# A two-layer hybrid block taken by halves of the tokens, with its norms by Newton's steps and its silu by tanh

## The chip, the core and the metric

The kernel runs on one core of a Trainium2 chip. The metric is the device time of one execution in microseconds. The core has five engines with queues of their own: TensorE (PE, with its weight loads shown apart as PEld), VectorE (DVE), ScalarE (ACT), GpSimd (POOL) and SyncE (SP), which issues most of the loads. An engine takes its instructions in order and waits at semaphores for the others.

## What is computed

A first block (attention beside a state-space layer, then a feed-forward of retrieved experts) takes 512 tokens of width 1024. Nothing of it is changed. Its output goes through the second block, two layers of this:

```python
def hybrid_layer(x, ...):
    x = x + 0.5 * swiglu(rmsnorm(x, ffn1_norm), ffn1_gate, ffn1_up, ffn1_down)
    z = rmsnorm(x, mix_norm) @ w_in
    (aq, ak, av, iq, ik, iw, bq, bk, bv, bg, br, cu, dcq, dckv, dkpe) = jnp.split(z, ...)
    y_a = dsa_mixer(...)    # attention on the 256 keys that an index scores highest
    y_b = gla_mixer(...)    # gated linear attention in chunks of 64, with a carried state
    y_c = conv_mixer(...)   # depthwise convolution of 31 taps, causal
    y_d = mla_mixer(...)    # attention with keys and values from a low-rank latent
    x = x + jnp.concatenate([y_a, y_b, y_c, y_d], axis=-1) @ w_out
    x = x + 0.5 * swiglu(rmsnorm(x, ffn2_norm), ffn2_gate, ffn2_up, ffn2_down)
    return x

def swiglu(x, w_gate, w_up, w_down):
    return (jax.nn.silu(x @ w_gate) * (x @ w_up)) @ w_down
```

The width of the feed-forward is 2816 = 22 chunks of 128. All four mixers are causal: a token sees only tokens at or before its own place.

## The kernel before

The residual `hT` lies feature-major: 128 partitions, 8 chunks of features, 512 tokens. Every large product is made in three matmuls (`mm3`, L192; the matmuls are L195, L196 and L197): a float32 number is split into `hi`, a 12-bit part, and `lo`, the rest, and the product is hi·hi + hi·lo + lo·hi. The split of an activation is an ACT copy and a DVE subtraction (L180, L181). Weights are loaded in blocks of up to 1024 columns and split too (`lw`, L996: SP issues the load, ACT casts in L1006, DVE or POOL subtracts in L1007). The raw block, its `hi` and its `lo` have two buffers each.

A layer (L960) runs a feed-forward, the mixers and a second feed-forward, each over all 512 tokens.

The feed-forward (`ffn`, L1010) takes the 22 chunks of its width in groups of 8, 7 and 7. For each chunk it makes the gate's and the up's product (8 chunks of features, 24 matmuls of 512 columns each). Both outputs are multiplied by 1/rms of the token (L1030, L1032: the norm's gain is in the input already, by `scaled`, L968, and 1/rms is left to the outputs), silu is taken by ACT, the two are multiplied and split. After a group its down products follow, 8 of them, each added to the residual (L1044). All that is 1584 matmuls for a feed-forward, 6336 for the four.

The mixers (`mixer`, L1047) make 23 blocks of `w_in` (`proj`, L1053; evicted with 1/rms by DVE in `keep`, L1063) and run the four mixers' steps as the list ORDER (L816) names them: `conv` (L1538: 30 DVE instructions for each of two chunks), `index` and `topk`, `mla`, `gla`, `dsa`. Then comes `w_out`, 8 outputs in two parts. The lo of most of these weights is made on POOL.

The squares' sum of a norm (`rows_rstd`, L978) is made by ACT squares and POOL additions (L986), then a product with a matrix of ones (L989); 1/sqrt is ACT's Ln and Exp. Silu and sigmoid are ACT functions of another table, so that ACT loads tables again and again.

A scheduler puts the instructions of each engine in order by what they depend on and by the place where the program issues them; tags with their number of buffers (TAGS, L813) bound how far ahead work may go.

## Time and profile before

| | us |
|---|---|
| median of 3 runs | 3860.31 |
| lowest and highest | 3859.98, 3862.52 |
| span of the profiled execution, which is its own time | 3860.0 |
| first block, to about | 1727 |
| layer 1: feed-forward, mixers, feed-forward, to about | 2099, 2419, 2792 |
| layer 2: the same, to about | 3165, 3482, 3860 |

The times of the stages are read off the first and last matmul of each. A matmul's own duration in the trace is longer than the spacing from one start to the next, because the engine overlaps them; so a stream of matmuls is read by its starts. In a table by windows, each engine's busy time is followed by the number of its instructions; then come the granted clock of PE as a share of the full 2.4 GHz, the busy share of the DMA engines and what they moved.

### The profile page before, as it was taken

How to read it: one execution, taken by the hardware profiler on the slowest of the kernel's cores; microseconds unless marked ns; L12 is line 12 of the kernel's file. 1: busy time of each engine (PE TensorE's matmuls, PEld its weight loads, DVE VectorE, ACT ScalarE, POOL GpSimd, SP SyncE). 2: the span in 40 equal slices, each digit the busy share in tenths (PEclk: the TensorE clock that was granted, in tenths of full speed). 3: DMA queues.
4: the chain of work that ended last, by engine and by line, in shares of the span. 5: the costliest groups of instructions: out<-in, count | busy, mean ns of one | idle time of the engine just before them, and what ended most of it. 6: DMA issues, size and time to landing. Idle time of an engine off the chain costs nothing.

```text
span 3860.0 us, 48976 instructions
## 1 busy us (share of the span) xinstructions
PE 3668.7 (95%) x17973; PEld 3082.1 (80%) x17973; DVE 2662.7 (69%) x4895; ACT 1464.7 (38%) x2614; POOL 1207.6 (31%) x949
## 2 busy tenths in 40 slices
PE   7798989879999999989999899999999998999999
PEld 6666877779999999978887577788788875767887
DVE  9668988677899999974445997444444449974343
ACT  3253369533333333332223446322332234463222
POOL 4424756466566666650001321000100013210000
PEclk8899989999999999999999999999999999999999
DMA  4213224766788888852232111223322232112333
GB/s 116 76 39 102 75 104 189 249 218 220 269 313 309 305 307 303 310 190 93 94 94 89 63 44 49 89 94 95 94 92 94 93 93 63 44 44 93 93 93 98
DMA packets 215889, 530.06 MB, mean 137 GB/s; under 512 B 23137, under 2 KB 124065, under 8 KB 197473
## 3 DMA queue, kind: packets, MB, share of 16 engines
q1 hardware_dynamic: 191632, 389.37, 31.2%
q0 software_dynamic: 18944, 134.75, 9.4%
q10 hardware_dynamic: 5072, 2.81, 0.3%
q8 instruction: 142, 2.33, 0.2%
q14 instruction: 99, 0.80, 0.1%
HBM read 495.51 MB, written 30.18 MB: 136 GB/s over the span
## 4 chain that ended last, share of the span: by engine, by line
PE 71%; DVE 8%; ACT 3%; DMA 2%; POOL 1%; issue 1%; SPq 0%; ACTq 0%; POOLq 0%; DVEq 0%
PE ps L197 13%; PE ps L195 13%; PE ps L196 13%; PE V L197 4%; PE V L196 4%; PE V L195 4%; PE S L196 3%; PE S L197 3%; PE S L195 3%; DVE cv L1538 2%; PE G L1749 2%; ACT gst L1750 1%; PE win L197 1%; PE win L195 1%; PE win L196 1%
## 5 line engine op out<-in xcount | busy, mean ns | idle before, releaser
L1006 ACT ACTIVATE wh<-wr 128x1024 fp32r<-128x1024 f32 (+1 forms) x334 | 347.2, 1040 | 1073.1 <-PE ps L196 748.9
L197 PE MATMUL ps<-x,wl 128*128 128x512 f32 x1408 | 559.7, 397 | 0.0
L195 PE MATMUL ps<-x,wh 128*128 128x512 f32 x1408 | 559.3, 397 | 0.0
L196 PE MATMUL ps<-x,wh 128*128 128x512 f32 x1408 | 559.3, 397 | 0.0
L1809 POOL TENSOR_TENSOR big<-vr,big 128x384 fp32r<-128x384 f32 (+1 forms) x384 | 406.3, 1083 | 146.6 <-ACT big L1808 90.9
L986 POOL TENSOR_TENSOR s<-s,s 128x512 f32<-128x512 f32 x42 | 68.5, 1631 | 1170.0 <-ACT s L984 1158.7
L1007 DVE TENSOR_TENSOR wl<-wr,wh 128x1024 fp32r<-128x1024 f32 (+1 forms) x288 | 343.8, 1194 | 44.2 <-ACT wh L1006 37.6
L195 PE MATMUL V<-ah,big 128*128 128x384 f32 x1024 | 346.2, 339 | 20.1 <-ACT big L1808 8.6
L196 PE MATMUL V<-al,big 128*128 128x384 f32 x1024 | 347.7, 340 | 11.0 <-DVE al L181 10.8
L197 PE MATMUL S<-pxh,ul 128*128 128x384 f32 x1024 | 348.5, 340 | 7.6 <-POOL ul L1767 7.6
L197 PE MATMUL V<-ah,big 128*128 128x384 f32 x1024 | 347.4, 340 | 6.0 <-POOL big L1809 6.0
L195 PE MATMUL S<-pxh,uh 128*128 128x384 f32 x1024 | 348.4, 340 | 0.0
L196 PE MATMUL S<-pxl,uh 128*128 128x384 f32 x1024 | 347.7, 340 | 0.0
L195 PEld LDWEIGHTS ps<-x,wh 128*128 128x128 f32 x1408 | 265.7, 189 | 66.4 <-ACT ml L944 1.1
L197 PEld LDWEIGHTS ps<-x,wl 128*128 128x128 f32 x1408 | 265.6, 189 | 65.4 <-issue 0.7
L196 PEld LDWEIGHTS ps<-x,wh 128*128 128x128 f32 x1408 | 265.7, 189 | 65.2 <-issue 0.5
L1871 POOL DMA_INDIRECT rows<-in_uv_dram,gidx x128 | 221.1, 1728 | 205.6 <-DVE acc L1880 162.6
L1873 DVE SCALAR_TENSOR_TENSOR rows<-rows,hn 128x1024 f32<-128x1024 f32 x128 | 280.4, 2214 | 4.7 <-DMA rows<-in_uv_dram,gidx 4.7
L195 PE MATMUL ps<-ml,wh 128*128 128x512 f32 x704 | 279.1, 396 | 0.0
L197 PE MATMUL ps<-ml,wl 128*128 128x512 f32 x704 | 279.1, 396 | 0.0
L1032 DVE TENSOR_TENSOR s<-ps,rs 128x512 f32<-128x512 f32 x88 | 60.9, 692 | 309.0 <-PE ps L197 309.0
L1044 DVE SCALAR_TENSOR_TENSOR hT<-ps,hT 128x512 f32<-128x512 f32 x96 | 66.4, 692 | 272.9 <-PE ps L197 272.9
(575 smaller groups left out, 8185.6 us busy)
## 6 DMA issues: line engine op xcount, KB each, us to landing
wr<-in_f_gu_dram SPq DMA_DIRECT2D x176, 512.0 KB
ur<-in_ut_dram SPq DMA_DIRECT2D x128, 512.0 KB
vr<-in_uv_dram SPq DMA_DIRECT2D x128, 384.0 KB
wr<-in_f_dn_dram SPq DMA_DIRECT2D x64, 448.0 KB
gates<-gst SPq DMA_DIRECT2D x12, 2048.0 KB
gt<-gates SPq DMA_DIRECT2D x32, 768.0 KB
wr<-in_w_dram SPq DMA_DIRECT2D x46, 512.0 KB
vr<-in_uv_dram SPq DMA_DIRECT2D x64, 256.0 KB
```

The lines of the kernel that those rows point to most:

```text
L195: mm(out, wh, xh, start=start, stop=False)
L196: mm(out, wh, xl, start=False, stop=False)
L197: mm(out, wl, xh, start=False, stop=stop)
L986: nc.gpsimd.tensor_tensor(sq, acc, sq, op=OP.add)
L1006: nc.scalar.activation(hi, raw, AF.Copy)
L1007: (eng or nc.vector).tensor_tensor(lo, raw, hi.bitcast(F32), op=OP.subtract)
L1044: V.scalar_tensor_tensor(x[:, m], ps, 0.5, x[:, m], op0=OP.mult, op1=OP.add)
L1538: V.scalar_tensor_tensor(a, hp[:, m, k:k + T], dw[:, m, k:k + 1], a, op0=OP.mult, op1=OP.add)
L1749: nc.tensor.matmul(ps[:, (t - t4) * P:(t - t4 + 1) * P], b, a, start=True, stop=True)
L1809: nc.gpsimd.tensor_tensor(vl, raw[:, k, :m], vh.bitcast(F32), op=OP.subtract)
L1871: nc.gpsimd.indirect_dma_start(r, None, self.A["uv"], bass.IndirectOffsetOnAxis(ap=self.gi[:, s:s + 1], axis=0))
L1873: self.tc.keep_in_program_order(V.scalar_tensor_tensor(r[:, :D], r[:, :D], 1.0, self.hn, op0=OP.mult, op1=OP.mult, accum_out=self.dot[:, 0 ...
```

## The change

Only the second block is changed. Its work is done for 256 tokens at a time. A layer issues: feed-forward 1 of half 0, mixers of half 0, feed-forward 1 of half 1, mixers of half 1, feed-forward 2 of half 0, feed-forward 2 of half 1. The mixers of half 1 use the keys, values, last columns of the convolution's input and last state that half 0 kept. Every half loads, casts and splits all weights again.

The norm is applied to the input ahead of the products (`normed`): ACT squares and POOL additions by half, two products with one column of ones (`ss`, L1014), 13 small DVE instructions (`tok_rstd`: a first guess from the number's bits, three Newton steps), an ACT copy that spreads the result (`rs`, one buffer), two transposes on PE (`rb`, L1021), and for each of the 8 chunks a DVE multiplication, an ACT copy and a DVE subtraction. Nothing is multiplied by 1/rms later; `w_in`'s outputs are evicted by ACT. Silu and sigmoid are made from tanh, whose missing halves are put into later factors. Weights of the feed-forward and of the mixers have tags of their own, with three raw buffers, two of hi and two of lo each; blocks of `w_in` are loaded in halves of 512 columns, their lo on POOL but for two blocks.

```diff
-TAGS = {"x": 16, "ml": 12, "ds": 7, "sm": 4, "sd": 4, "gl": 10, "r": 2, "t3": 1, "rg": 2, "cv": 2, "rs": 1}
-F_GRP = ((0, 8), (8, 15), (15, 22))
+F_GRP = ((0, 6), (6, 12), (12, 17), (17, 22))
+HW = T // 2
+TAGS = {"fx": (HW, 16), "mx": (HW, 16), "fh": (HW, 14), "fs": (HW, 4), "g1": (HW, 14), "rs": (HW, 1), "t3": (HW, 1),
+        "q": (HW, 6), "rg": (HW, 2), "cv": (HW, 2), "am": (T, 2), "sm": (T, 6), "s": (T, 2), "pt": (T, 2)}
+WTS = {"f": (1024, 3), "m": (512, 3)}
-    def layer(self, l, x):
+    def run(self, x):
+        for l in range(2):
...
+            for h in range(2):
+                self.ffn(l, 0, x, h)
+                self.mixer(l, x, h, kept)
+            for h in range(2):
+                self.ffn(l, 1, x, h)
+    def tok_rstd(self, ssq, n, scale=1.0):
...
+        V.tensor_scalar(m, ssq, 1.0 / n, EPS, op0=OP.mult, op1=OP.add)
+        V.tensor_copy(u, m.bitcast(I32))
+        V.tensor_scalar(u, u, -0.5, 1597463007.0, op0=OP.mult, op1=OP.add)
+        V.tensor_copy(r.bitcast(I32), u)
+        for s in (1.0, 1.0, scale):
+            V.scalar_tensor_tensor(u, r, -0.5 * s, r, op0=OP.mult, op1=OP.mult)
+            V.tensor_mul(u, u, m)
+            V.scalar_tensor_tensor(r, u, 1.5 * s, r, op0=OP.add, op1=OP.mult)
+    def rstd(self, sqs, n, g=1, bank=None):
...
+        r = self.tok_rstd(ps[:, :2 * g], n)
+        rb = self.mt("rs")
+        nc.scalar.activation(rb.rearrange("p (a m) -> p a m", a=2 * g), r.unsqueeze(2).to_broadcast([P, 2 * g, P // g]),
+                             AF.Copy)
+        ps = net.ps(bank, "rb")[:, :HW]
+        for i in range(2):
+            mm.transpose(ps[:, i * P:(i + 1) * P], rb[:, i * P:(i + 1) * P], net.c("ident"))
+    def normed(self, x, h, g, tag, bank):
...
+        r = self.rstd([acc], D, 1, bank)
+        for c in range(NCH):
+            y = self.mt("fs")
+            nc.vector.scalar_tensor_tensor(y, x[:, c, hs], self.gv(g, c), r, op0=OP.mult, op1=OP.mult)
+            out.append(self.split(y, tag))
-    def lw(self, dram, n, eng=None, tag=None):
+    def lw(self, dram, n, tag, eng=None):
...
+        raw, hi, lo = (w.tile([P, width], dt, tag=tag + t, name=self.net.nm(t), bufs=d)[:, :n]
+                       for t, dt, d in (("wr", F32, depth), ("wh", F32R, 2), ("wl", F32R, 2)))
     def ffn(...)
...
-                V.tensor_mul(s, ps[0], r)
-                nc.scalar.activation(s, s, AF.Silu)
-                V.tensor_mul(u, ps[1], r)
-                V.tensor_mul(u, u, s)
-                net.split(u, hh[-1], hl[-1])
+                t = self.mt("fs")
+                nc.scalar.activation(t, ps[:, :HW], AF.Tanh, scale=0.5)
+                V.scalar_tensor_tensor(t, t, 1.0, ps[:, :HW], op0=OP.add, op1=OP.mult)
+                u = self.mt("fs")
+                V.tensor_mul(u, t, ps[:, HW:])
+                hid.append(self.split(u, "fh"))
...
-                V.scalar_tensor_tensor(x[:, m], ps, 0.5, x[:, m], op0=OP.mult, op1=OP.add)
+                V.scalar_tensor_tensor(x[:, m, hs], ps, 0.25, x[:, m, hs], op0=OP.mult, op1=OP.add)
     def mixer(...)
...
+            ps = net.ps("pd", "win")[:, :HW]
+            for c0 in (0, 4):
+                wh, wl = (a.rearrange("p (c m) -> p c m", c=4) for a in self.lw(
+                    self.A["w2"][l, b][:, c0 * P:(c0 + 4) * P], 512, "m", V if b in (14, 16) else G))
+                for c in range(4):
+                    net.mm3(ps, (wh[:, c], wl[:, c]), xn[c0 + c], c0 + c == 0, c0 + c == NCH - 1)
-            V.tensor_mul(t, proj(b), rx)
+            nc.scalar.activation(t, proj(b), AF.Copy)
```

On PE, at the end of layer 1's first feed-forward, there stood the last down products, of 512 columns, and behind them the first block of `w_in`:

```order
L195 MATMUL ps_19746<-ml_19533,wh_19741 128x512
L196 MATMUL ps_19746<-gl_19534,wh_19741 128x512
L197 MATMUL ps_19746<-ml_19533,wl_19742 128x512
L195 MATMUL win_19845<-x_19781,wh_19770 128x512
L196 MATMUL win_19845<-x_19789,wh_19770 128x512
L197 MATMUL win_19845<-x_19781,wl_19771 128x512
```

At the end of feed-forward 1 of half 0 there now stand the last down products (`dn`), of 256 columns, the sums of squares, the transposes of 1/rms, and then the first block of `w_in`:

```order
L195 MATMUL dn_19806<-fh_19635,wh_19801 128x256
L196 MATMUL dn_19806<-fh_19636,wh_19801 128x256
L197 MATMUL dn_19806<-fh_19635,wl_19802 128x256
L1014 MATMUL ss_19851<-cst,fs_19848 128x1 x2
L1021 MATMUL rb_19870<-cst,rs_19868 128x128 x2
L195 MATMUL win_19923<-mx_19875,wh_19925 128x256
L196 MATMUL win_19923<-mx_19876,wh_19925 128x256
L197 MATMUL win_19923<-mx_19875,wl_19926 128x256
```

The norm's two products with `ss` and `rb` stand between the stages now, and no product of another half does.

On PE, at the end of the mixers of half 0, the last products of `w_out` (`wo`) are followed by the transposes of the next norm, and only then by the first gate product (`gu`) of the other half's feed-forward:

```order
L195 MATMUL wo_22082<-mx_21644,wh_22077 128x256
L196 MATMUL wo_22082<-mx_21645,wh_22077 128x256
L197 MATMUL wo_22082<-mx_21644,wl_22078 128x256
L1021 MATMUL rb_22138<-cst,rs_22136 128x128 x2
L195 MATMUL gu_22189<-fx_22143,wh_22191 128x256
L196 MATMUL gu_22189<-fx_22144,wh_22191 128x256
L197 MATMUL gu_22189<-fx_22143,wl_22192 128x256
```

All 1584 matmuls of a half's feed-forward stand in one piece on PE, behind all products of the mixers of the half before; only at the end of the mixers of half 1 do a few of the next feed-forward's rows stand among them.

On DVE, where a group's gate and up products end and its down products begin, the evictions of gate and up (L1030, L1032, L1033), the lo of weights (L1007) and the first eviction of a down product (L1044) stood thus:

```order
L1030 TENSOR_TENSOR s_18031<-ps_17975,rs_17473 128x512
L1007 TENSOR_TENSOR wl_18043<-wr_18041,wh_18042 128x1024
L1032 TENSOR_TENSOR s_18032<-ps_18006,rs_17473 128x512
L1033 TENSOR_TENSOR s_18032<-s_18032,s_18031 128x512
L1007 TENSOR_TENSOR wl_18075<-wr_18073,wh_18074 128x1024
L181 TENSOR_TENSOR gl_18038<-s_18032,ml_18037 128x512
L1044 SCALAR_TENSOR_TENSOR hT<-ps_18047,hT 128x512
```

and now (L1057 is the lo of a weight block, L988 that of an activation, L1079 and L1081 the gate with its tanh and the product with the up, L1091 the first eviction of a down product):

```order
L1057 TENSOR_TENSOR wl_18549<-wr_18547,wh_18548 128x768
L988 TENSOR_TENSOR fh_18474<-fs_18471,fh_18473 128x256
L1057 TENSOR_TENSOR wl_18575<-wr_18573,wh_18574 128x768
L1079 SCALAR_TENSOR_TENSOR fs_18538<-fs_18538,gu_18477 128x256
L1081 TENSOR_TENSOR fs_18541<-fs_18538,gu_18477 128x256
L988 TENSOR_TENSOR fh_18544<-fs_18541,fh_18543 128x256
L1091 SCALAR_TENSOR_TENSOR hT<-dn_18553,hT 128x256
```

The lo of the first two down blocks stands ahead of the last chunk's gate now; before, the second's stood behind that chunk's gate and up.

## Rows read from the trace of the kernel before

**Rows 1.** The page's part 1: busy time, share of the span, instructions.

```profile
PE 3668.7 (95%) x17973; PEld 3082.1 (80%) x17973; DVE 2662.7 (69%) x4895; ACT 1464.7 (38%) x2614; POOL 1207.6 (31%) x949
```

**Rows 2.** Windows: both mixers, a feed-forward, the first block, the mixers' two ends.

```profile
2098.60:2419.70 321.10, 298.12 (x1404) 216.07 (x1404) 266.70 (x543) 158.67 (x327) 80.33 (x34) 0.96 0.17 54
2423.00:2790.00 367.00, 366.62 (x1563) 294.48 (x1564) 158.25 (x186) 106.05 (x128) 8.74 (x7) 1.00 0.30 93
3164.00:3483.50 319.50, 299.49 (x1411) 215.47 (x1410) 271.56 (x541) 159.21 (x327) 75.36 (x34) 0.97 0.17 56
1200.00:1600.00 400.00, 400.00 (x2309) 399.89 (x2308) 387.62 (x469) 140.58 (x313) 261.47 (x205) 1.00 0.86 308
2098.60:2116.50 17.90, 16.70 (x70) 12.81 (x70) 7.65 (x9) 8.83 (x10) 1.76 (x1) 1.00 0.23 76
2385.00:2419.70 34.70, 34.70 (x177) 27.12 (x176) 19.03 (x27) 20.20 (x38) 9.30 (x6) 1.00 0.24 77
```

**Rows 3.** Timeline of PE in a feed-forward: start, duration, engine, line, tiles (first and 53rd start).

```profile
2999.71 0.39 PE L195 MATMUL ps<-x,wh 128*128 128x512 f32 x1
...
3011.89 0.40 PE L196 MATMUL ps<-gl,wh 128*128 128x512 f32 x1
```

**Rows 4.** Timeline of PE in the first block, products of 264 columns (first and 17th).

```profile
174.00 0.28 PE L195 MATMUL proj<-xh,wh 128*128 128x264 f32 x1
...
175.95 0.28 PE L196 MATMUL proj<-xl,wh 128*128 128x264 f32 x1
```

**Rows 5.** Weight loads by tile: minimum, median and maximum ns.

```profile
L195 PEld LDWEIGHTS proj<-xh,wh x128: 186/188/337, 19.1 to 175.7; 128*128 128x128 f32 x128
```

**Rows 6.** Timeline of PE in the first block, products of 128 columns and what follows.

```profile
559.82 1.50 PE L1749 MATMUL G<-ga,gb 128*128 128x128 f32 x12
561.08 0.42 PE L195 MATMUL S<-pxh,uh 128*128 128x384 f32 x1
```

**Rows 7.** Timeline of PE behind an idle stretch, 512 columns (first and 12th).

```profile
66.30 0.76 PE L195 MATMUL proj<-xh,wh 128*128 128x512 f32 x1 [11.32 <-DVE ph L392]
...
71.13 0.63 PE L197 MATMUL proj<-xh,wl 128*128 128x512 f32 x1
```

**Rows 8.** Groups by form, a feed-forward: busy us, mean ns, idle before.

```profile
L1007 DVE TENSOR_TENSOR wl<-wr,wh 128x1024 fp32r<-128x1024 f32 x51 | 62.4, 1223 | 6.0 <-ACT wh L1006 5.9
L1006 ACT ACTIVATE wh<-wr 128x1024 fp32r<-128x1024 f32 x51 | 54.1, 1061 | 190.4 <-PE ps L196 139.1 <-issue 51.3
...
L1007 DVE TENSOR_TENSOR wl<-wr,wh 128x896 fp32r<-128x896 f32 x16 | 17.5, 1092 | 1.5
...
L1006 ACT ACTIVATE wh<-wr 128x896 fp32r<-128x896 f32 x16 | 15.3, 955 | 51.4 <-PE ps L196 40.4 <-issue 11.0
```

**Rows 9.** Groups by form, layer 1's mixers.

```profile
L1007 POOL TENSOR_TENSOR wl<-wr,wh 128x1024 fp32r<-128x1024 f32 x23 | 59.3, 2577 | 182.9 <-ACT wh L1006 138.8 <-PE win L197 24.7 <-ACT pt L1201 11.9
L1538 DVE SCALAR_TENSOR_TENSOR cv<-hp,dw,cv 128x512 f32<-128x512 f32 x60 | 56.3, 966 | 0.3
...
L1063 DVE TENSOR_TENSOR ds<-win,rs 128x512 f32<-128x512 f32 x7 | 4.8, 682 | 0.7 <-PE win L197 0.7
...
L1295 DVE SCALAR_TENSOR_TENSOR sd<-dsa,rq,sd 128x256 f32<-128x256 f32 x4 | 1.8, 483 | 0.5 <-PE dsa L1294 0.3
...
L1353 DVE TENSOR_TENSOR sd<-ml,tr 128x256 f32<-128x256 f32 x4 | 1.7, 420 | 0.0
L1339 ACT ACTIVATE s<-ml 128x256 f32<-128x256 f32 x4 | 1.7, 416 | 0.2
```

**Rows 10.** Lines by source: the convolution's, and a small norm's (minimum, median, maximum ns).

```profile
L1538 DVE SCALAR_TENSOR_TENSOR cv<-hp,dw,cv x120: 725/741/2923, 2116.5 to 3261.4; 128x512 f32<-128x512 f32 x120
...
L217 DVE TENSOR_TENSOR tr<-tr x7: 159/176/899, 177.2 to 3386.1; 128x16 f32<-128x16 f32 x4, 128x32 f32<-128x32 f32 x3
```

**Rows 11.** Timeline of POOL in layer 1's mixers, then of PE behind it.

```profile
2101.00 1.76 POOL L986 TENSOR_TENSOR s<-s,s 128x512 f32<-128x512 f32 x1 [3.12 <-ACT s L984]
...
2102.82 1.12 PE L989 MATMUL ps<-s,cst 128*128 128x512 f32 x2 [1.20 <-POOL s L986]
```

More of the change, by code (lines that the diff above doesn't have):

```diff
@@ L950, in mt, with keep_tile @@
     def mt(self, tag, dt=F32):
-        return self.p.tile([P, T], dt, tag=tag, name=self.net.nm(tag), bufs=TAGS[tag])
-    def mts(self, tag, n, dt=F32R):
-        return [self.mt(tag, dt) for _ in range(n)]
+        width, n = TAGS[tag]
+        return self.p.tile([P, width], dt, tag=tag, name=self.net.nm(tag), bufs=n)
+    def keep_tile(self, name, shape, bufs=1):
+        return self.p.tile([P] + shape, F32, tag=name, name=self.net.nm(name), bufs=bufs)
     def gv(self, name, i=None):
@@ new lines, in rstd @@
+    def rstd(self, sqs, n, g=1, bank=None):
+        net, nc = self.net, self.nc
+        mm, mat = nc.tensor, net.c("ones")[:, 0:1] if g == 1 else net.c("bo64")[:, 0:P:64]
+        ps = net.ps(bank, "ss")
+        for i in range(2):
+            for k, sq in enumerate(sqs):
+                mm.matmul(ps[:, i * g:(i + 1) * g], sq[:, i * P:(i + 1) * P], mat, start=k == 0, stop=k == len(sqs) - 1)
+        r = self.tok_rstd(ps[:, :2 * g], n)
[3 more added lines that the diff above has]
+        ps = net.ps(bank, "rb")[:, :HW]
+        for i in range(2):
+            mm.transpose(ps[:, i * P:(i + 1) * P], rb[:, i * P:(i + 1) * P], net.c("ident"))
+        return ps
@@ L985, in rows_rstd, with squares @@
+    def squares(self, chunks):
+        out = [self.mt("s")[:, :HW] for _ in chunks]
+        for sq, c in zip(out, chunks):
+            self.nc.scalar.activation(sq, c, AF.Square)
+        return out
+    def normed(self, x, h, g, tag, bank):
+        net, nc = self.net, self.nc
+        hs = slice(h * HW, h * HW + HW)
+        acc = None
+        for c in range(NCH):
+            sq = self.mt("fs")
+            nc.scalar.activation(sq, x[:, c, hs], AF.Square)
             if acc is not None:
@@ L1312, in mla_in @@
[L1312 to L1319 removed]
+            r = self.rstd(self.squares(raw), 128 * len(raw))
+            for c, y in enumerate(raw):
+                V.scalar_tensor_tensor(y, y, self.gv(g, c), r, op0=OP.mult, op1=OP.mult)
+                lat.append(self.split(y, "g1"))
@@ L1387, in mla_in @@
-        return Q, K, kv, rq
-    def mla(self, j, qkv, ya):
+        rq = w.tile([P, 2, 4], F32, tag="rqd", name=net.nm("rqd"), bufs=2)
+        V.tensor_copy(rq.rearrange("p a b -> p (a b)"), self.tok_rstd(psq[:, :8], 96, 96 ** -0.5))
+        for i in range(4):
+            ps = net.ps()[:, :HW]
+            for k in range(2):
+                nc.tensor.transpose(ps[:96, k * P:(k + 1) * P], kf[k][:, i], ident)
+            nc.scalar.activation(kept["K"][:96, i, hs], ps[:96], AF.Identity, scale=self.gv("dk1")[:96])
@@ L1390, in mla @@
+        return Q, rq
+    def mla(self, j, h, qs, kept, ya):
         net, nc = self.net, self.nc
         V = nc.vector
-        Q, K, kv, rq = qkv
-        n = (j + 1) * P
-        ts = slice(j * P, n)
-        sm = self.mts("sm", 4, F32)
-        for h in range(4):
+        Q, rq = qs
+        n, lj = (j + 1) * P, j - 2 * h
+        ts, ls = slice(j * P, n), slice(lj * P, (lj + 1) * P)
+        sm = [self.mt("sm") for _ in range(4)]
+        for i in range(4):
             ps = net.ps()
-            nc.tensor.matmul(ps[:, :n], Q[h][:96, ts], K[h][:96, :n], start=True, stop=True)
-            r = rq[:, j, h:h + 1]
+            nc.tensor.matmul(ps[:, :n], Q[i][:96, ls], kept["K"][:96, i, :n], start=True, stop=True)
+            r = rq[:, lj, i:i + 1]
@@ L1461, in gla_in, with gla @@
             ke.append(k)
-        return b3, kt, dl, qe, qi, ke
-    def gla(self, parts, bq, bk, vt):
-        net, nc, w, p = self.net, self.nc, self.w, self.p
+        return kt, dl, qe, qi, ke
+    def gla(self, half, parts, bq, bk, vg, kept):
+        net, nc, w = self.net, self.nc, self.w
         V = nc.vector
-        b3, kt, dl, qe, qi, ke = parts
+        kt, dl, qe, qi, ke = parts
         qs = 32 ** -0.5
-        S = p.tile([P, 8, P], F32, tag="gS", name=net.nm("gS"))
-        V.memset(S[:, 0], 0.0)
-        for c in range(7):
+        S = self.keep_tile("gS", [3, P])
+        if not half:
+            kept["S"] = self.keep_tile("gS4", [P])
+        st = [kept["S"] if half else self.zero] + [S[:, c] for c in range(3)] + [kept["S"]]
+        for c in range(3 if half else 4):
             i, hs = c // 2, slice((c % 2) * 64, (c % 2) * 64 + 64)
@@ L1499, in gla @@
         for m in range(2):
-            po = net.ps()
+            po = net.ps()[:, :HW]
             pr = slice(m * 64, m * 64 + 64)
-            for i in range(4):
+            for i in range(2):
                 for h in (2 * m, 2 * m + 1):
                     rows = slice((h % 2) * 64, (h % 2) * 64 + 64)
-                    nc.tensor.matmul(po[rows, i * P:(i + 1) * P], vt[:, i, 256 + h * 64:256 + (h + 1) * 64],
+                    nc.tensor.matmul(po[rows, i * P:(i + 1) * P], vg[:, i, h * 64:(h + 1) * 64],
@@ L1906, in net_kernel @@
     b2 = Block2(net, ctx)
-    for l in range(2):
-        b2.layer(l, hT)
+    b2.run(hT)
     for c in range(NCH):
```

503 lines of the change are left out of this document (242 added, 261 removed).

## Prediction

> **What bounds the kernel now.** I read four views in this order. The busy times say that PE carries the time, 95% of the span [rows 1]. The windows say where it doesn't: in a feed-forward PE is busy for 366.62 of 367.00 us, but in the mixers' 321 and 320 us DVE is busy for 266.7 and 271.6 while PE has 298 and 299 with many waits [rows 2]. The timelines of PE give the price of a matmul by its columns, from start to start: 512 columns (3011.89 − 2999.71) / 52 = 0.2342 us [rows 3], 264 columns (175.95 − 174.00) / 16 = 0.1219 [rows 4]. The groups by form give the price of what DVE and ACT do [rows 8, 9]. So the feed-forwards, 1485 us in all, can only become shorter by fewer or denser matmuls, of which the change makes neither. What it could win is in the mixers: two times some 50 us in which DVE is idle, if PE worked on the other half's feed-forward while DVE works on the mixers.
>
> **Does PE do that?** The order printed above says no. All 1584 matmuls of a half's feed-forward stand behind the last `wo` product of the half before, on an engine that takes its rows in order. The mixers of half 0 wait for their own softmax and top-k as before, with nothing of the other half to fill the wait; only the tail of half 1's mixers gets some gate products. So I price the change as if each stage ran alone, at half width, twice.
>
> **1. Spacing of the feed-forwards' matmuls.** 6336 of 512 columns become 12672 of 256. Between 264 and 512 columns a straight line gives 0.1219 − 8 × (0.2342 − 0.1219) / 248 = 0.1183 us [rows 3, 4]. 12672 × 0.1183 − 6336 × 0.2342 = 1499 − 1484 = +15 us. At 0.1171, half of the wide one, it is 0; at 0.1219 it is +61. Weight loads, one per matmul, become twice as many and are no bound by that: the products of 264 columns load as often, each load lasts 188 ns [rows 5], and yet they start every 122 ns, so loads overlap each other.
>
> **2. Weights.** Each block is loaded, cast and split once per half. A gate block of 1024 columns gives 24 matmuls, 2.84 us; in that time DMA has to bring 512 KB, twice the 93 GB/s that a feed-forward draws now, and the first block draws 308 [rows 2], so with three raw buffers I price loads at nothing. The hi and lo slots come free with the last matmul: cast 1.06, lo 1.22 [rows 8] and 0.1 of hand-overs, 2.4 us inside 2.84. A down block of 5 chunks is tightest: by the slopes of rows 8 (0.83 ns a column on ACT, 1.02 on DVE) its 640 columns take 0.74 + 0.83 and hand-overs, 1.7, inside 15 × 0.1183 = 1.77. Priced at nothing as long as this holds; if each of the 256 down blocks were 0.2 us late, +51.
>
> **3. The turn from up to down.** In the last group of 8 chunks of 512 columns, the first down product had 7 × 3 × 0.234 = 4.9 us of earlier chunks to cover the last one's silu and split. Now, by the order on ACT and DVE, behind the last up matmul come: the cast of the second down block 0.85, its lo 0.96, then the gate 0.48, the product 0.42, the hi 0.42 and the lo 0.42 [rows 8, 9], 3.55 and five hand-overs of some 0.06 (the 2102.82 − 2101.00 − 1.76 of [rows 11]): 3.85. Against that stand 15 or 12 matmuls of earlier chunks, 1.8 or 1.4 us, and the first of the last chunk's needs hi alone. About 2.0 us is left, at 4 groups × 8 halves = 32 places: +64. If the cast stands behind the tanh after all, near 0; without any cover +80.
>
> **4. Seams.** A norm ahead of the products is a chain: eviction 0.48, square 0.42, POOL's addition half of 1.76 [rows 11], 13 small DVE instructions of 0.176 [rows 10] = 2.3, the spread 0.42, the transposes 0.2 (two products of 128 columns [rows 6]), then for the first chunk 0.48 + 0.42 + 0.42, with hand-overs some 6.5 us. After that DVE gives a chunk every 0.90 us where PE uses one in 3 × 0.118 = 0.355, for 7 more chunks: +3.8. Before, 1/rms was beside the products. Three times a feed-forward follows another; the input is there, but `ss` stands behind the last down product: 4.6 + 3.8, about 8 us. Two times one follows half 0's mixers with only `rb` behind: about 5. Together +34, from 15 (only `rb` exposed everywhere) to 60. The seams ahead of the mixers are in the next term.
>
> **5. The mixers.** DVE bounds them, so its work is counted, per layer. Now 269 (mean of two [rows 2]). The 23 evictions with 1/rms go to ACT: −23 × 0.682 = −16. Newton: 10 norms a half × 13 × 0.176 × 2 halves = 46, less 3 of small instructions that it replaces: +43. Some 140 instructions of 512 columns become twice as many of 256, each pair 2 × 0.42 − 0.68 = 0.16 dearer [rows 9]: +22. The norm's input: 16 × (0.48 + 0.42) − 8 × 0.74 = +8. The lo on DVE: 24 of 512 columns at 0.68 for 8 of 1024 at 1.22: +7. Together 333. Then POOL: the convolution's median is 0.741 [rows 10] but its mean in the mixers 0.966 [rows 9], 13.5 us over 60 of them beside 80 us of POOL [rows 2]: the two get in each other's way. POOL will have some 100 halves of blocks × 1.29 and the additions, about 150 us: +12. So 345. Idle time of DVE is now 54 and 48, of which the two ends have 10.2 and 15.7 (17.90 − 7.65 and 34.70 − 19.03 [rows 2]); ends come twice: 51 + 26 = 77. 345 + 77 = 422 in place of 320, +102 a layer, **+204**. The low end is DVE's 333 with the idle 51 of now: +64 a layer, +128. The high end is every wait twice, 345 + 102: +127 a layer, +254. I take the middle value since dependent chains (top-k, softmax, scan) come per half, but the blocks of `w_in` between them don't get longer.
>
> Sum against the profiled execution's 3860.0 (the median of the runs is 0.3 above it): 3860 + 15 + 64 + 34 + 204 = 4177; forecast **4175 us**. With all low ends 4003, with all high ends 4315. ACT loses its table loads and gains evictions; it is half busy in the mixers and no term.
>
> **Rivals.**
> B, the halves pack: if the rows between the stages wait less than I think (`w_in` blocks of one half run while DVE ends the other's, turns half covered), the mixers cost 360 a layer (+80), turns 32, seams 20, spacing 15: 4007. For it speaks that DVE's work ahead of `rb` doesn't wait for PE; against it that `wo` needs all four mixers and stands ahead of every product of the other half.
>
> C, the clock falls: behind an idle stretch of 11.32 us matmuls of 512 columns start every (71.13 − 66.30) / 11 = 0.44 us [rows 7], the 1.2 GHz level, where 0.234 is the rate at 2.4. The mixers now show a granted clock of 0.96 and 0.97 [rows 2]; thinner work with longer waits could keep it low. PE's 298 us a layer would become up to 559, 137 above the 422; at two thirds of the stretch some +85 a layer, +170: 4345. The Trainium skill, "TensorE: Matmul & The Clock Gate", section "Why this matters for your kernels", warns that matmuls thin in M let the clock go up and down. No row here tells width from waiting: the products of 264 columns in rows 4 run at the fast rate's spacing while they are back to back, which speaks against width alone.
>
> D, on the other side, faster: the spacing falls to what 128 columns show, (561.08 − 559.82) / 12 = 0.105 [rows 6], and B holds too: 12672 × 0.105 − 1484 = −153, and 80 + 32 + 20: 3839. It decides at a spacing below 0.1064, where (with B) gains and losses are equal. Against it: 128 columns are half the work and cost 0.105, 264 cost 0.122, so 256 under 0.11 would need a break in the line.
>
> E, weight loads become the bound: at 188 ns apiece [rows 5] 12672 cost 2382, +898 in place of +15: 5060. Against it rows 4, as said. A milder form comes from the same page of the Trainium skill, section "Back-to-back issue gap": sustained 81 ns a matmul at 128 columns and 131 at 512. By a straight line I estimate 98 at 256, so that halving the width costs 1.49 times the feed-forwards' time, +727, some 4890. The trace does not agree: it shows 234 ns at 512 and 122 at 264, near a half.
>
> **How the numbers follow.** My forecast 0.70, B 0.12, C 0.12, D 0.04, E 0.02. The likeliest is 4175. The range from 4000 to 4360 takes in B, C and the ends of the forecast's terms and leaves D and E out. A measurement of this kernel tells some 0.2% from no change, 8 us. D is faster in most of its forms (0.03), the same in the rest (0.01); all others are slower, 0.96.
>
> **What would show it.** A feed-forward of a half should last 1584 × 0.1183 = 187 us and four stalls of about 2 us; 256-column matmuls should start every 0.118 us. DVE should be busy for about 165 to 172 us in each half's mixers, which should last about 211. The convolution's mean should be further over its median. Wrong would be: PE with gate products among the mixers' (then B), a granted clock under 0.9 in the mixers (C), a spacing under 0.11 (D) or over 0.13 (E), or down blocks that wait for their own lo (term 2).

## The result, and the profile after

The changed kernel takes 4318.5 us (median of 4 runs, 4308.9 to 4326.0) against 3861.0 (4 runs): 1.118 times as long, 95% interval 1.1165 to 1.1203. It is slower, as forecast, by 458 us where 315 were forecast; the time lies inside the range and near its upper end, 4 us above the forecast's own terms with all their high ends (4315).

The stages, from the first to the last matmul of each, say where the 458 us are:

| | before | forecast | after |
|---|---|---|---|
| first gate product of the second block starts | 1723.5 | no change | 1735.3, +12 |
| the feed-forwards (4, or 8 halves) | 1495.7 | +79 (terms 1 and 3) | 1610, +114 |
| seams ahead of a feed-forward | in the stages | +34 | +26 |
| both mixers, the seam ahead of them included | 636.8 | +204 | 944, +307 |

The windows of the changed kernel for half 0's mixers (from the end of one feed-forward to the start of the next), the feed-forward of half 1 and half 1's mixers, all of layer 1, answer to [rows 2]. The columns are the same: the stretch and its length, then busy time and instructions of PE, PEld, DVE, ACT and POOL, then PE's granted clock, the DMA share and GB/s.

```profile
1937.04:2163.11 226.07, 172.70 (x1072) 150.16 (x1072) 162.65 (x452) 104.85 (x265) 78.00 (x63) 0.82 0.26 81
2163.11:2366.08 202.97, 195.84 (x1584) 192.61 (x1584) 122.93 (x186) 89.07 (x133) 5.95 (x7) 0.99 0.55 166
2366.08:2617.30 251.22, 193.12 (x1188) 160.47 (x1188) 208.98 (x528) 123.29 (x287) 77.53 (x61) 0.84 0.23 72
```

The feed-forward has its 1584 products and nothing else: as the order said, the stages stand one behind the other. Its length, 203 us, is mostly products. Their spacing is read from PE's timeline:

```profile
2249.42 0.28 PE L195 MATMUL gu<-fx,wh 128*128 128x256 f32 x1
...
2255.18 0.28 PE L195 MATMUL dn<-fh,wh 128*128 128x256 f32 x1
```

48 products lie between these two starts: 5.76 / 48 = 0.1200 us, where [rows 3, 4] had given 0.1183. Right behind a norm it is twice that: the products go in threes, one three for each chunk of the input, every (2166.13 − 2164.67) / 2 = 0.73 us. The clock isn't the reason at this place, since it is granted in full; DVE makes a chunk (its multiplication and its lo, L1045 and L988) every 0.73 us (PE's timeline, its window, DVE's timeline):

```profile
2164.67 0.28 PE L195 MATMUL gu<-fx,wh 128*128 128x256 f32 x1
...
2166.13 0.28 PE L195 MATMUL gu<-fx,wh 128*128 128x256 f32 x1
```

```profile
2163.00:2166.20 3.20, 2.04 (x10) 1.43 (x10) 3.20 (x9) 1.72 (x6) 1.00 (x1) 1.00 0.59 163
```

```profile
2164.20 0.47 DVE L1045 SCALAR_TENSOR_TENSOR fs<-hT,vec,rb 128x256 f32<-128x256 f32 x1
2164.59 0.41 DVE L988 TENSOR_TENSOR fx<-fs,fx 128x256 fp32r<-128x256 f32 x1
2164.93 0.47 DVE L1045 SCALAR_TENSOR_TENSOR fs<-hT,vec,rb 128x256 f32<-128x256 f32 x1
```

Six of the eight feed-forwards stand behind a norm that PE waits for, and lose 2.5 to 3.8 us at their start in this way, 18 in all; the two behind half 1's mixers lose nothing. The table counts this in the feed-forwards, the forecast in its seams.

At a turn from up to down the first product of the group's last chunk waits, and then the group's third down block waits for its own lo (start, duration, idle before, releaser):

```profile
2256.86 0.28 PE L197 MATMUL dn<-fh,wl 128*128 128x256 f32 x1
2258.08 0.36 PE L195 MATMUL dn<-fh,wh 128*128 128x256 f32 x1 [0.94 <-DVE fs L1081]
...
2261.37 0.39 PE L197 MATMUL dn<-fh,wl 128*128 128x256 f32 x1 [0.30 <-DVE wl L1057]
```

In the mixers neither PE nor DVE is busy all the time. What PE waits for in half 0's (us in total, times, longest), and the first of these waits in PE's timeline:

```profile
PE mlain L1021 <- ACT rs L1017: 17.1, 2, 9.9
PE win L197 <- POOL wl L1057: 6.8, 12, 2.3
PE index L1291 <- ACT s L1293: 6.2, 1, 6.2
PE ss L1014 <- POOL fs L1039: 4.3, 1, 4.3
PE rb L1021 <- ACT rs L1017: 3.1, 1, 3.1
```

```profile
2007.38 0.95 PE L1014 MATMUL mlain<-cst,s 128*128 128x1 f32 x8
2018.22 0.69 PE L1021 MATMUL mlain<-cst,rs 128*128 128x128 f32 x2 [9.89 <-ACT rs L1017]
```

DVE's timeline in that wait shows the norm's steps (`tr`) each queued behind an instruction of the convolution (`cv`) or of top-k (`am`, `m`), so that 13 steps of 0.15 us last 6 us, from 2011.8 to 2017.7, where their own durations make 2:

```profile
2013.46 0.16 DVE L1000 CAST tr<-tr 128x2 int32<-128x2 f32 x1
2013.53 0.08 DVE L1309 MATCH_VALUE_LOAD am<-m,am 128x8 f32 x1
2013.60 0.41 DVE L1309 MATCH_REPLACE8 am<-m,am 128x256 f32<-128x256 f32 x1
2013.93 0.15 DVE L1002 SCALAR_TENSOR_TENSOR tr<-tr 128x2 f32<-128x2 f32 x1
2013.99 0.48 DVE L1603 SCALAR_TENSOR_TENSOR cv<-hp,dw,cv 128x256 f32<-128x256 f32 x1
2014.39 0.15 DVE L1003 TENSOR_TENSOR tr<-tr 128x2 f32<-128x2 f32 x1
2014.46 0.42 DVE L1308 MAX8 m<-am 128x8 f32<-128x256 f32 x1
2014.80 0.14 DVE L1004 SCALAR_TENSOR_TENSOR tr<-tr 128x2 f32<-128x2 f32 x1
```

Behind such waits the granted clock is at half, here also in a slice in which PE is busy for 14.6 of 15 us (windows behind that wait):

```profile
2020.00:2035.00 15.00, 7.14 (x25) 5.59 (x26) 13.00 (x52) 4.96 (x15) 1.27 (x1) 0.50 0.01 2
2035.00:2050.00 15.00, 14.60 (x67) 13.88 (x66) 11.59 (x35) 4.91 (x11) 5.07 (x4) 0.50 0.22 70
2050.00:2065.00 15.00, 12.60 (x93) 11.27 (x91) 2.25 (x10) 9.87 (x18) 6.72 (x6) 0.99 0.33 107
```

So four explanations of the mixers stood open: DVE's total of work (theory V, the forecast's), chains of short dependent steps (S, and W where they queue behind long instructions), the clock (C), and that the halves were never laid beside each other (P). All runs below are single measurements unless an interval is given. The changed kernel's own runs spread from 4309 to 4326, and on the chips that were used the kernel before took from 3856 to 3869, so that differences under some 15 us say little. Of a single mixer stage, differences of 5 us say nothing: in e4 below, whose edit is in the feed-forward, the two of layer 1 are 5 us shorter and 5 us longer.

### The profile page after: what moved, and what is told of

Same layout as the page of the kernel before. It is cut to its first block, busy times and chain, and to the rows that moved or that the text cites. A ratio compares the mean times of both kernels' runs of the same rounds, so it can differ in the third digit from the quotient of the medians.

```text
span 4318.5 us, 70494 instructions
## 1 busy us (share of the span) xinstructions
PE 3869.9 (90%) x26033; PEld 3609.2 (84%) x26033; DVE 3217.0 (74%) x6539; ACT 1880.6 (44%) x3601; POOL 1364.0 (32%) x1152
## 3 DMA queue, kind: packets, MB, share of 16 engines
q14 instruction: 137, 1.12, 0.1%
## 5 line engine op out<-in xcount | busy, mean ns | idle before, releaser
L1056 ACT ACTIVATE wh<-wr 128x1024 fp32r<-128x1024 f32 (+3 forms) x868 | 739.2, 852 | 1056.1 <-PE gu L196 406.7
L1057 DVE TENSOR_TENSOR wl<-wr,wh 128x1024 fp32r<-128x1024 f32 (+3 forms) x656 | 695.8, 1061 | 556.4 <-ACT wh L1056 554.0
L196 PE MATMUL gu<-fx,wh 128*128 128x256 f32 x2816 | 803.4, 285 | 2.3 <-DVE fx L988 1.4
L195 PE MATMUL gu<-fx,wh 128*128 128x256 f32 x2816 | 798.8, 284 | 6.8 <-ACT fx L987 6.7
L197 PE MATMUL gu<-fx,wl 128*128 128x256 f32 x2816 | 800.4, 284 | 4.5 <-DVE wl L1057 4.5
L195 PEld LDWEIGHTS gu<-fx,wh 128*128 128x128 f32 x2816 | 536.3, 190 | 9.3 <-ACT fx L987 8.8
L197 PEld LDWEIGHTS gu<-fx,wl 128*128 128x128 f32 x2816 | 535.9, 190 | 8.0 <-DVE wl L1057 6.3
L196 PEld LDWEIGHTS gu<-fx,wh 128*128 128x128 f32 x2816 | 532.5, 189 | 5.6 <-DVE fx L988 5.2
L1057 POOL TENSOR_TENSOR wl<-wr,wh 128x512 fp32r<-128x512 f32 x212 | 285.3, 1350 | 601.9 <-ACT wh L1056 526.0
L195 PE MATMUL dn<-fh,wh 128*128 128x256 f32 x1408 | 395.7, 285 | 32.0 <-DVE fs L1081 32.0
L197 PE MATMUL dn<-fh,wl 128*128 128x256 f32 x1408 | 398.7, 284 | 10.9 <-DVE wl L1057 10.9
L196 PE MATMUL dn<-fh,wh 128*128 128x256 f32 x1408 | 394.8, 282 | 0.0
L195 PEld LDWEIGHTS dn<-fh,wh 128*128 128x128 f32 x1408 | 263.0, 188 | 38.2 <-issue 33.9
```

Of the source, the lines that this page charges most:

```text
L195: mm(out, wh, xh, start=start, stop=False)
L196: mm(out, wh, xl, start=False, stop=False)
L197: mm(out, wl, xh, start=False, stop=stop)
L1056: nc.scalar.activation(hi, raw, AF.Copy)
L1057: (eng or nc.vector).tensor_tensor(lo, raw, hi.bitcast(F32), op=OP.subtract)
```

## Were the halves ever beside each other?

**e1.** The norm of the next feed-forward is issued ahead of the mixers:

```diff
+            xn = self.normed(x, 0, "f1", "fx", "pa")
             for h in range(2):
-                self.ffn(l, 0, x, h)
+                self.ffn(l, 0, x, h, xn)
+                xn = self.normed(x, 1 - h, ("f1", "f2")[h], "fx", "pa")
                 self.mixer(l, x, h, kept)
...
```

> Edit: the norm of the next half's feed-forward is issued ahead of a half's mixers instead of behind them; nothing else. On PE some 230 of the 1584 products of that feed-forward then stand among the mixers' products. Theory P (the halves don't overlap because the program issues, and so orders, one behind the other): each of the four mixers hides about 230 x 0.120 = 27 us of a feed-forward, and the clock falls less, so 80 to 130 us less than the changed kernel's 4318: 4190 to 4240. Theory V (DVE is the bound of the mixers, and the lo of the feed-forward's weights, which DVE makes, only pushes the mixers' own work back): within 30 us of 4318.

4278.5 us, 40 less. It is between the two, nearer to V's bound. The mixers of layer 1 now take 221 and 244 us from their first `w_in` product to their last of `w_out` (215 and 242 before that edit). Half 0's hold 230 products of the feed-forward that stand outside otherwise, half 1's only 115, and 96 more stand ahead of each one's first `w_in` product. From the end of one feed-forward to the end of the next, 21 and 18 us are won around half 0's mixers and 2 and 5 around half 1's. So the 27 us a stage that theory P expected came near in half 0 alone.

**e11.** The second block's order by simulated time, alone:

```diff
-    b2.run(hT)
+    with tc.block(name="second", schedule_with_timeline_sim=True):
+        b2.run(hT)
```

> Edit to the changed kernel: the second block's order by simulated time, the norm of the next half's feed-forward left behind the mixers. On PE about 170 of 1584 products of that feed-forward then stand among the mixers' last ones. If e2 gained by the two edits together (the norm early so that there is work to place, the timed order to place it): a quarter to a half of e2's 197 us, 4220 to 4270. If the timed order alone makes a better order within the mixers: 4150 or less.

4382.7 us, 64 more: a miss of both expectations. The mixers of layer 1 take 235 and 280 us:

```profile
1960.20:2195.60 235.40, 185.24 (x1242) 165.68 (x1243) 171.75 (x462) 112.61 (x279) 79.35 (x60) 0.84 0.25 85
2386.50:2666.10 279.60, 209.62 (x1356) 178.25 (x1357) 216.16 (x526) 129.96 (x297) 78.72 (x59) 0.85 0.22 72
```

These stretches hold some 175 products of the next feed-forward, some 21 us. With the feed-forwards, which are shorter by as much, half 0's mixers lose nothing (2 us less and 3 more in the two layers), and half 1's lose 20 us in each layer. The rest is 10 us ahead of the block's first product and some 3 us in each feed-forward that stands alone. So the order that the simulated time makes is worse for half 1's mixers as such; why is not shown.

**e8.** The same edit to the kernel before, around both layers:

> Edit to the kernel before, at full width and without the change: the second block's order is made by simulated time instead of by issue. In its mixers PE was idle for 23 and 20 us of 321 and 320, and that is all that any better order can win there. Expected: 0 to 30 us less than before's 3861, if the simulated time fits the chip; if it misjudges POOL against DVE, up to 30 more.

3958.7 us beside 3869.2 for the kernel before on that chip, 90 more, another miss. Its two mixers take 358 and 363 us in place of 320 and 317, at a granted clock of 0.90:

```profile
2112.10:2470.00 357.90, 315.03 (x1400) 228.68 (x1399) 279.67 (x540) 166.89 (x331) 72.74 (x33) 0.90 0.14 47
3216.20:3579.00 362.80, 316.89 (x1399) 230.26 (x1398) 278.96 (x537) 166.59 (x331) 73.46 (x32) 0.90 0.14 46
```

DVE's busy time rises by 13 and 7 us only; the rest is waiting and a lower clock. The order of the same work is worth some 40 us a stage here.

**e2.** Both edits, e1's and e11's, together:

> Edit: as the run with the early norm, and the second block's order is made by the scheduler's simulated time, as the first block's is, in place of the order of issue. On PE the feed-forward's products then stand in pieces of 1 to 28 all through the mixers. Theory P: a mixer of a half and a feed-forward of the other take together what PE needs at full clock, 1584 x 0.120 = 190 us and about 150 us, 340 in place of 426 now: four times 86 less, some 3980, and a granted clock near 1.0 in these stretches. Theory V: DVE needs 122 us for the feed-forward and 160 to 205 for the mixers, in order, so that weights of the feed-forward wait behind the mixers' chains; the pair takes 400 or more and the whole 4200 or more.

4121.7 us, 197 less. **e12** writes the same intent into the program, without simulated time: a feed-forward is a generator and moves on by a chunk or a down block, or a few, behind each step of the other half's mixers.

```diff
...
         for s in ORDER:
             steps[s]()
+            for _ in range(SIDE.get(s, 1)):
+                next(side, None)
...
```

> Edit: the program itself issues the other half's feed-forward between the steps of the mixers, a chunk of gate and up or a down block (or several) behind each step, with its norm ahead of the mixers; the order stays that of issue. On PE the feed-forward then stands in some 60 pieces among the mixers' products. Theory P: as e2 or better, since every wait of the mixers has products to stand in for it and the mixers' own order is untouched: a pair of mixers and feed-forward in 340 to 380 us in place of 426, 3980 to 4120 in all. Theory B (PE's own work is the floor: the kernel before had PE idle for only 43 us in both mixers, and halves make the feed-forwards 114 us longer): even then no less than 3900, and slower than the 3861 of before. Theory V (the feed-forward's casts and splits, in the same queues of ACT and DVE as the mixers' chains, hold both back): 4200 or more.

4141.9 us (4134.4 to 4144.8, 4 runs; 1.072 of before, 1.0707 to 1.0742), 177 less. These are the windows of its two stretches of mixers and feed-forward in layer 1:

```profile
1965.40:2316.50 351.10, 332.10 (x2549) 310.63 (x2548) 256.77 (x588) 180.95 (x372) 74.60 (x58) 0.98 0.44 144
2344.60:2726.90 382.30, 360.35 (x2657) 325.94 (x2656) 300.64 (x652) 197.77 (x390) 76.12 (x57) 0.97 0.41 132
```

Theory P holds: where the program issues the halves beside each other, they do lie beside each other, and 177 us come back, where the mixers had lost 307. It also shows the end of that road, as theory B had it. PE is busy for 332 of 351 and 360 of 382 us, at a clock of 0.98 and 0.97. The same share of the kernel before, half of a mixer stage and half of a feed-forward, is (320 + 374) / 2 = 347 us. PE has no less to do at half width, so even a perfect overlap would give about the time of before, not less (no run shows one). No version here beats the kernel before.

## What bounds a mixer stage?

**e7.** The convolution with 2 of its 31 taps; the other 29 products of each channel are left out.

```diff
-            for k in range(1, 31):
+            for k in range(1, 2):
```

> Edit: the convolution is made with 2 of its 31 taps, so 29 of 30 DVE instructions are left out for each of two chunks in each half: 58 x 0.70 = 41 us of DVE a half, 163 in all. Theory V (DVE's busy time sets the mixers' end): 130 to 165 us less, 4155 to 4190. Theory S (chains of short dependent steps over several engines set it, and the convolution mostly fills DVE's idle time): under 70 us less.

4279.5 us, 39 less. Half 0's mixers go from 226 to 207 us, half 1's stay at 252, with DVE now busy for 130 and 175, in place of 163 and 209:

```profile
1936.25:2143.03 206.78, 165.89 (x1073) 143.88 (x1073) 129.78 (x394) 104.55 (x265) 76.48 (x63) 0.86 0.27 88
2345.17:2597.10 251.93, 200.68 (x1188) 165.47 (x1187) 175.41 (x470) 123.60 (x287) 75.54 (x61) 0.82 0.22 72
```

The taps left out last 162 us by their own durations, as expected, but DVE's busy time in the four stages falls by 133 only (33 or 34 in each of layer 1), since durations of neighbouring instructions overlap in the trace. Theory V falls: 39 of 133 us came back, and in half 1 a stage without 34 us of DVE's work has not moved. In layer 2 half 0's stage goes from 223 to 205 and half 1's from 246 to 244.

**e10.** The same edit to the kernel before, with the same products left out:

> Edit to the kernel before: the convolution is made with 2 of its 31 taps; 58 DVE instructions of 0.97 us are left out in each layer, 112 us in all. If the mixers before were bound by DVE, as the forecast says: some 100 us less than 3861, about 3760, each mixer stage about 265 us. If PE's own work of 298 us a layer bounds them and DVE hardly shows: at most the 43 us in which PE was idle, 3815 or more.

3827.0 us beside 3856.4 for the kernel before on that chip, 29 less, where DVE is busy for 220 and 220 us in place of 267 and 272, 98 less. PE is busy for 291 of 302 us in the mixers now:

```profile
2098.50:2400.10 301.60, 291.20 (x1399) 211.07 (x1398) 220.38 (x485) 157.68 (x326) 72.72 (x34) 0.99 0.18 58
3147.00:3447.40 300.40, 290.72 (x1400) 210.25 (x1399) 219.84 (x482) 157.80 (x326) 69.40 (x33) 0.99 0.17 58
```

So DVE wasn't the bound before either. PE's own 298 us in [rows 2] were the floor, and the 43 us that PE was idle in both mixers were all that an overlap could win. About half of this idle time did hang on the convolution: in e10's two windows PE is idle for 20 us, and its work takes 16 us less at a clock of 0.99 in place of 0.96.

**e6.** One Newton step in place of three; 1/rms is less exact by it.

```diff
-        for s in (1.0, 1.0, scale):
+        for s in (scale,):
```

> Edit: one Newton step instead of three, 7 small DVE instructions a norm instead of 13; 1/rms is less exact by that. 48 norms x 6 x 0.2 us = 58 us of DVE go. Theory S (the mixers wait for the norms' chains, whose steps queue behind long instructions): 6 of 13 steps of 17 us a half at the latents, and as much in the other norms of a mixer and the seams: 60 to 100 us less. Theory V (only DVE's busy time counts): at most 50 less. Theory 0 (the norms are hidden): within 10 us.

4257.1 us, 61 less, for 44 × 6 = 264 instructions (the kernel has 44 such norms, not 48): 0.23 us for each one left out. DVE's busy time in the whole execution falls by 54 us, so its whole price came back, where e7's 140 us gave 39. Half 0's mixers take 209 us and half 1's 240:

```profile
1931.40:2140.50 209.10, 164.80 (x1078) 143.29 (x1079) 160.83 (x404) 105.50 (x270) 77.04 (x62) 0.86 0.27 87
2338.60:2578.90 240.30, 194.83 (x1188) 161.93 (x1188) 195.39 (x468) 123.59 (x288) 78.45 (x61) 0.85 0.23 75
```

DVE's busy time falls by 2 and 14 us there, the stages by 17 and 11. Theory S holds by e6 and e7 together: a microsecond of the norms' small steps costs about a microsecond of the whole, one of the convolution a third or nothing. It does not hold everywhere: layer 2's half 1 takes 246 us with either number of Newton steps and 244 without the taps, and what sets that stage is not shown.

**e3.** Top-k and the convolution are pinned behind the DVE work issued ahead of them:

```diff
-        for _ in range(16):
-            V.max(m8, acc)
+        for k in range(16):
+            top = V.max(m8, acc)
+            if not k:
+                self.tc.keep_in_program_order(top)
...
+            self.tc.keep_in_program_order(first)
```

(`first` is the first instruction of a chunk of the convolution.)

> Edit: the first DVE instruction of each top-k and of each chunk of the convolution is pinned behind the DVE work issued ahead of it, so that the 13 small steps of the latents' norms no longer alternate with top-k's and the convolution's long instructions. Theory W (PE waits for Newton's steps, each queued behind one or two long instructions on DVE: 17 and 18 us a half at the products of the latents, and the clock falls to half behind that): these waits shrink to some 10 us, and with the clock 40 to 60 us go: 4260 to 4280. Theory V (DVE's total of work sets the mixers' end, in whatever order): within 15 us of 4318, the wait moves elsewhere.

4347.2 us, 29 more: a miss. The wait at the latents shrinks a little,

```profile
PE mlain L1021 <- ACT rs L1017: 12.9, 2, 9.0
```

from 17.1, and half 0's stage is what it was (225.6 us against 226.1). Half 1's takes 270 in place of 251: its top-k, some 40 us of DVE's work in a chain, starts 93 us later now, and a softmax of `mla` stands behind it on DVE, for which PE waits 18 us in one piece:

```profile
2563.05 3.78 PE L1458 MATMUL mla<-K,q 96*128 96x512 f32 x4 [18.04 <-DVE sm L1462]
```

Queueing behind long instructions lengthens the norms, but putting the norms first only moves the wait to top-k's chain. W is no explanation on its own.

**e5 and e9.** PE is given products that nobody reads, to keep its clock up in the norms' waits. e5 writes them into the bank of the sums of squares (a bank is a part of the memory in which PE leaves its results):

```diff
+        for _ in range(6):
+            mm.matmul(ps[:, HW:], net.c("ident"), self.rope[:, :HW], start=True, stop=True)
         r = self.tok_rstd(ps[:, :2 * g], n)
```

> Edit: in every norm, between the sums of squares and the transposes of 1/rms, PE makes 6 products of 256 columns in float32 whose result nobody reads, some 2.6 us at full clock; they stand where PE waits for the small steps. Theory C (the clock that falls in these waits is a large part of what the forecast missed): stages behind a norm start at full clock, which gives back about 3 us in each of 8 feed-forwards and 10 to 15 in each of 4 mixers: 40 to 80 us less than 4318. Rival D (PE in the mixers waits for DVE anyway, so a faster clock only lengthens its waits): the mixers stay within 5 us each, only the feed-forwards' starts gain, 10 to 25 us in all.

4417.0 us, 99 more, and no answer: DVE's first step waits until these products are done (DVE's timeline, whose idle stretch ends with PE),

```profile
1952.53 0.16 DVE L997 TENSOR_SCALAR tr<-ss 128x2 f32<-128x2 f32 x1 [5.67 <-PE ss L1016]
```

so each norm became longer by them. e9 gives them a bank of their own, and only places where PE waits:

```diff
+        def fill(k):
+            dm = net.ps("pd" if bank == "pa" else "pa", "dm")[:, :HW]
+            for i in range(k):
+                d = mm.matmul(dm, net.c("ident"), self.rope[:, :HW], start=True, stop=True)
+                if not i:
+                    self.tc.keep_in_program_order(d)
+        if bank == "pd":
+            fill(7)
         ps = net.ps(bank, "ss")
...
+        if bank or net.ptag == "pb":
+            fill(5 if bank else 10)
```

> Edit: as e5, but the products that nobody reads go to a bank of their own, so that the norm's reading doesn't wait for them, and they stand only where PE has nothing else to do: 7 ahead of the sums of squares of a mixer's input norm, 5 behind the sums of every input norm, 10 behind the sums of the two latents' norms (some 0.47 us each at full clock, against waits of 4, 3 and 7 to 10 us). Theory C (what the forecast missed in the mixers is to a good part PE at half clock behind these waits): 3 us a feed-forward and 10 to 15 us a mixer come back, 4240 to 4280. Rival D (PE waits for the chains in any case): the granted clock in the mixers rises and the time stays within 15 us of 4318.

4306.2 us, 12 less, 3 us under the fastest of the changed kernel's own runs, and on a chip where the kernel before was 5 us faster too. The granted clock in half 0's mixers rises from 0.82 to 0.90, and the stage goes from 226 to 222 us; half 1's clock from 0.84 to 0.89 and its stage from 251 to 256, no more than e4 shows without a fill:

```profile
1932.30:2154.60 222.30, 180.64 (x1147) 153.96 (x1145) 164.79 (x452) 104.51 (x265) 78.97 (x63) 0.90 0.26 84
```

So the low clock is a companion of the waits more than a price of its own, as far as 0.90 shows. The fill doesn't reach every wait, and its own products take time; a clock of 1.0 throughout wasn't tried. At the start of a feed-forward it can be told: behind half 0's mixers e9 has the full clock (window below), and its first products still lose 2.5 us, since they wait for DVE's chunks.

```profile
2154.60:2158.00 3.40, 2.75 (x13) 1.85 (x13) 3.40 (x10) 2.16 (x6) 0.00 (x0) 1.00 0.21 74
```

## The turn from up to down

**e4.** The lo of each group's second down block on POOL:

```diff
-                          self.lw(self.A["f_dn"][l, i][:, o:o + n], n, "f"))
+                          self.lw(self.A["f_dn"][l, i][:, o:o + n], n, "f", nc.gpsimd if m == 1 else None))
```

> Edit: of each group of the feed-forward, the lo of the second down block is made on POOL instead of DVE. Theory T (as in the forecast: at each of the 32 turns from up to down the last chunk's gate waits on DVE behind that lo, 0.96 us): the wait of the first down product for the last chunk falls by up to 0.9 us, 20 to 30 us in all: about 4290. Rival: the chain of tanh, gate, product and split is what PE waits for, or POOL's slower lo (1.9 us) is late itself: within 10 us of 4318, or slower.

4314.8 us, 4 less, not to be told from none by the time. The waits of PE in one feed-forward show the edit at work: for the last chunk 1.9 us in four turns, where the changed kernel has 4.0 (first fence e4, second the changed kernel):

```profile
PE dn L195 <- DVE fs L1081: 1.9, 4, 0.6
```

```profile
PE dn L195 <- DVE fs L1081: 4.0, 4, 1.1
```

By the length of the eight feed-forwards that is 8 us. About half of the wait was the queue behind that lo, the other half the chain of gate, product and split.

## Why the prediction was right, and where it was wrong

**That PE doesn't lay the halves beside each other** was right, and it was the basis: 1584 products in one piece, seen in the order and now in the windows. e1, e2 and e12 show what the forecast didn't say, that this was for the issue order of a norm and a feed-forward alone, and worth 180 to 200 us.

**What bounds the kernel now** was wrong for the mixers. The forecast read DVE's 267 and 272 us as the bound because PE showed waits; e10 takes 46 and 52 us of DVE's work from the stages and gets 18 and 16 back, at which PE is busy for 291 of 302. And "two times some 50 us" of possible gain was read off DVE's idle time; it was PE's, 23 and 20.

**Term 1** (+15) was mis-sized: 0.1200 us and not 0.1183 makes 12672 × 0.1200 − 1484 = +37. Loads of 190 ns at twice the number were no bound, so E is out.

**Term 2** (nothing) was named with its sign of being wrong, down blocks that wait for their own lo, and the sign came true in part: the third down block of each group, 32 of 256, waits 0.5 us for its lo, 16 us in all. Other late blocks, mostly of the gate, make some 11 more. PE waits for no load directly, but behind one of these (at 2323.8 us) ACT's cast had waited 2.5 us for the load.

**Term 3** (+64): in a half's four turns PE's first product for the last chunk starts 1.1 or 1.2 us late, 4.6 together and 37 in the eight halves, where the sum had 2.0 a turn; the products right behind a late one add 7. The working holds in its proportion: e4 finds half of that wait behind the lo, and the sum had 0.96 of 2.0.

**Term 4** (+34) measured 42, if the seam and the slow start behind it are taken together as the forecast did. Between feed-forwards 7.7, 7.9 and 7.6 us pass from the last product to the first, where 4.6 were worked out, and 3 more are lost in the first chunks, where 3.8 were. Behind half 0's mixers it is 1.1 and 3.6, about the 5 of the forecast. DVE's pace of a chunk was 0.73 us and not 0.90.

**Not in the forecast:** the very first norm of the block costs 12. The feed-forwards' 114 are made of term 1 (37), the turns and late blocks (37 + 7 + 16 + 11), and the slow starts (18), less 12 that the kernel before lost at the starts of its own.

**Term 5** (+204) is the step that failed, by 103 us. By its own account both parts were too small: DVE's work is 163 + 209 = 372 us a layer, with a part of the next norm, against 345, and its idle time 63 + 42 = 106 against 77. But the account itself was the wrong one, since it took the stage as DVE's work plus its idle time. By e7 the work of the convolution counts in a part only, 39 of 133 us, and by e6 the norms' steps count in full: the stage is a chain through all engines, and such a chain comes once per half. The high end of the term, every wait twice, gave +254 and was still under the 307 measured. So the total is inside the range by some luck: the range reached up to 4360 for rival C, whose mechanism carried little of the time, as far as e9 shows.

**POOL beside the convolution** went as said: the median of a tap is 0.477 us now, its mean in half 0's mixers 0.739 and in half 1's 0.667. The trace shows that POOL is the reason: of the 240 taps, the 156 beside which POOL had no instruction lasted 0.49 us at most, and the 84 others 1.12 on average (half 0, half 1, both layers):

```profile
L1603 DVE SCALAR_TENSOR_TENSOR cv<-hp,dw,cv 128x256 f32<-128x256 f32 x60 | 42.0, 739 | 0.2
L1603 DVE SCALAR_TENSOR_TENSOR cv<-hp,dw,cv 128x256 f32<-128x256 f32 x60 | 37.6, 667 | 0.2
L1603 DVE SCALAR_TENSOR_TENSOR cv<-hp,dw,cv x240: 460/477/1583, 1963.0 to 3734.8; 128x256 f32<-128x256 f32 x120
```

(0.262 + 0.190) × 60 = 27 us a layer, against 13.5 + 12 in the forecast. By e7 such microseconds count in a small part only.

**Rivals.** C's sign came true, a clock of 0.82 to 0.87 in the mixers, and its mechanism didn't carry the time, as far as a clock of 0.90 can tell: e9 raises the clock and leaves the time. Its price didn't follow from its working either: two thirds of 137 are 91, not 85. B's premise, that the halves pack by themselves, didn't come true. D fell by the spacing of 0.1200; its 0.105 of [rows 6] was read off plain float32 products (L1749), which aren't those of `mm3`, and its turning point is 0.1067, not 0.1064. The Trainium skill's "TensorE: Matmul & The Clock Gate", section "Back-to-back issue gap", gives 81 ns at 128 columns and 131 at 512; this kernel's 120 ns at 256 and 234 at 512 are near a half of each other, and so the feed-forwards grew by 8%, not by half.

## What to carry to other kernels

Before an overlap is built, look at how long the engine that it is to fill is idle: here PE's 43 us in both stages were the most that could be won, whatever DVE's busy share was, and halving the width cost more than that in the feed-forwards alone. Here PE overlapped two pieces of work only where the program (e12), or a scheduler by simulated time (e2), put them in turns; a norm issued behind the other work was enough to undo it (e11). And a stage made of dependent steps over several engines is priced by its chain, once per piece into which it is cut, more than by the busy time of one engine: take some work out of the engine that seems to be the bound before believing that it is.

## What the runs showed of the chip that had not been expected

- An instruction of half the width costs well over half: a tap of the convolution 0.477 us at 256 columns against 0.741 at 512 [rows 10].
- PE's clock stayed at 0.50 for a slice of 15 us in which PE was busy for 14.6, behind two idle stretches of 9.9 and 7.3 us; in the next slice it was 0.99.
- A chunk's pace on DVE, 0.73 us, and not the clock, set the start of a feed-forward behind a norm.
- The order by simulated time made both kernels slower, by 64 and 90 us, and helped only where there was independent work to place (e2).
